# Third and fourth Strassen product exchanged in the later three token blocks of the first input phase of a pooling-mixer kernel

## Chip, cores and metric

The kernel runs on one core of a Trainium2 chip. The metric is the device time of one execution in microseconds (us); lower is better. The engines are named as in the profile: PE (matrix multiply), PEld (its weight load), DVE (vector), ACT (scalar), POOL (GpSimd) and SP, which here only issues DMAs. Each engine runs its own instructions strictly in order, so an instruction that waits holds up everything behind it on its engine.

## What is computed

With these sizes there is one layer, and it is the pooling mixer: 4096 tokens of 1024 channels.

```python
normed = rms_norm(x, norm_w)
u, gate = split(normed @ in_w, 2)            # 1024 -> 2048
pooled[g] = trailing_mean(u[g], (2, 4, 8, 16)[g]) - u[g]      # 4 groups of 256 channels
y = (pooled @ group_w + group_b) * scale * silu(gate)
out = rms_norm(x + y @ out_w, final_norm_w)
```

All arrays are float32. The group map is folded into the input weights at the start, and the pooling works on the result.

## The kernel before, in words

**Three phases.** The list `steps` (lines 949 to 951) holds them one behind the other. Phase "a" multiplies the normalised input by half of the input weights (512 gate columns and 512 folded value columns), in four blocks of 1024 tokens; phase "b" does the same for the other half of the weights from operands that phase "a" saved in HBM (`sd`); phase "o" is the output projection with the residual and the final norm, in eight blocks of 512 tokens.

**Seven products a block.** Each block is a 2x2 block product done by Strassen-Winograd in seven products, P1 to P7, each of 512x512x512. An operand is used as a high part and a low part (float32 split in two float32r numbers), and a product is the sum of three: high by high, high by low, low by high. So `product_in` (line 576) issues 2 halves h of the inner dimension x 4 channel tiles x 2 x 3 = 48 matmuls of 128x128 by 128x512, into four PSUM banks. In P1 the four banks are finished one after the other; in all other products half h=0 goes over all four banks first, then half h=1, so that bank 0 is finished after 5/8 of the product and bank 3 at its end. P1, P2, P7 and P4 use banks 0 to 3, P6, P5 and P3 use banks 4 to 7 (`bank_of`, line 574, and `sets_of`, line 976). P2 adds to what P1 left in banks 0 to 3, and P6, P5 and P3 add to a copy of it that ACT makes in banks 4 to 7.

**Operands.** The input block is in four quarters, "11", "12", "21", "22" (two token halves by two channel halves), each of two tiles of 128x1024 (512 KB). In phase "a" each tile is loaded from the transposed input by SP (`load_x`, line 480), multiplied on DVE by the token's reciprocal root mean square (`normalize`, line 454, traced as L148), and combined on DVE (`add` L142, `sub` L145): "21" becomes 11-21, the operand of P7; a new pair "2" becomes 22-21, the operand of P6; 11+2 is that of P5, 12-2 (`form_s4`, line 548) that of P3. `split` (line 153) then writes one of four operand buffers `op`: ACT writes the high part (L151), DVE the low part, source minus high (L145, `op<-st,op`). In phase "a" the operands of P1, P2, P7 and P4 are also saved to `sd`, each by a DMA that ACT issues (L476).

**Order around the change.** The order of one block is `ORDER_IN` = P1, P2, P6, P7, P5, P4, P3. In the loop from line 1193 on, step n loads for step n+3, forms the operand of step n+2, splits the operand of step n+1 and runs product n. In block b > 0 of phase "a", the step of P1 first normalises all four tiles of 21 and 22 (`normalize_a2`, line 526, called at line 1212), then forms P6's operand (four subtractions, `form_in`), and then splits P2's operand. Where `normal` (line 1213) holds, `form` comes behind the split instead. `evict_in` (line 699) empties the banks: P2's by ACT with SiLU into two tiles, P6's and P7's by ACT copies, P5's and P4's by DVE additions. `pool` (line 617) does the trailing means of an earlier product pair on DVE, multiplies by the gate and stores the result to `yd` (L685, issued by SP). Squares for the next block's norms run on ACT (L407), and the reciprocal roots go through HBM (`rd`) to be spread over partitions (L420, L452, issued by POOL). `save_t3` (line 273, called in block 2 behind P6) makes a weight difference that phase "b" needs.

Tiles come from two pools (`st`, `vt`), handed out oldest first, so what is given back when decides which tile is used next. A scheduler in the framework chooses the order on each engine from the program order; `issue_after` holds an instruction behind a named one.

**At the end** (lines 1259 to 1280) stand 36 matmuls behind the last product: four groups of nine with different access patterns, into banks that nothing reads.

Of the kernel before, what the change touches and what calls it, by code (L numbers as in the profile page):

```python
# [15 lines left out]
P = 128  # L16
# [4 lines left out]
NB = S // TB  # L21
NK = D // P
TO = 512
NBO = S // TO
# [5 lines left out]

P1, P2, P3, P4, P5, P6, P7 = range(1, 8)
ORDER_IN = (P1, P2, P6, P7, P5, P4, P3)
ORDER_OUT = (P1, P7, P6, P2, P5, P4, P3)


# [25 lines left out]
def kernel(  # L61
# [32 lines left out]
    nc = tc.nc  # L94
# [14 lines left out]
    w = {i: new_w(i) for i in (P1, P2, P6, P7)}  # L109
# [28 lines left out]
    def give(ap):  # L138
        next(p for p in (st, vt, early, early5) if id(ap) in p.used).give(ap)
# [4 lines left out]
    def sub(dst, a, b):  # L144
        return nc.vector.tensor_tensor(out=dst, in0=a, in1=b, op=ALU.subtract)  # L145
# [188 lines left out]
    latest = [None]  # L334
# [119 lines left out]
    def normalize(b, half, u):  # L454
        mul(u, u, rstd[b][:, half].unsqueeze(1).to_broadcast([P, 2, H]))
# [24 lines left out]
    def load_x(b, half, kh):  # L480
        us = []
        for h in range(2):
            u = take()
            k = 4 * kh + 2 * h
            nc.sync.dma_start(out=u, in_=xt[2 * b + 1 - half, :, k : k + 2, :])
            us.append(u)
        return us

    def load_saved(b, i):
        us = []  # L490
        for h in range(2):
            u = take()
            nc.sync.dma_start(out=u, in_=sd[b][i][h])
            us.append(u)
        return us

    def load_in(q, b, i):
        s = xs[b]
        if i == P1:
            s["11"] = load_saved(b, P1) if q else load_x(b, 0, 0)  # L500
        elif i == P2:
            s["12"] = load_saved(b, P2) if q else load_x(b, 0, 1)
        elif i == P6:
            s["21"] = load_saved(b, P7) if q else load_x(b, 1, 0)
            s["22"] = load_saved(b, P4) if q else load_x(b, 1, 1)

    def form_in(q, b, i):

        s = xs[b]
        if i in (P1, P2):  # L510
            if q == 0:
                for u in s["11" if i == P1 else "12"]:
                    normalize(b, 0, u)
        elif i == P6:
            s["2"] = [take() for _ in range(2)]
            for h in range(2):
                if q == 0:
                    sub(s["21"][h], s["11"][h], s["21"][h])
                sub(s["2"][h], s["22"][h], s["21"][h])
        elif i == P5:  # L520
            for h in range(2):
                add(s["11"][h], s["2"][h], s["11"][h])
            for u in s.pop("2"):
                give(u)

    def normalize_a2(b):
        for h in range(2):
            normalize(b, 1, xs[b]["21"][h])
            normalize(b, 1, xs[b]["22"][h])
        give(rstd.pop(b))  # L530

    def split_in(q, b, i):
        s = xs[b]
        key = {P1: "11", P2: "12", P6: "2", P7: "21", P5: "11", P4: "22", P3: "12"}[i]
        later = q == 0 and b == 0 and i in (P1, P2)
        t = split_halves(s[key], None if q or later else sd[b].get(i), b == 0)
        if later:
            stores.extend(zip(sd[0][i], s[key]))
        if i == P6 and (q or b):
            form_s4(b)  # L540
        if i not in (P1, P2, P6):
            for u in s.pop(key):
                give(u)
        return t
# [401 lines left out]

    steps = [("a", b, i) for b in range(NB) for i in ORDER_IN]
    steps += [("b", b, i) for b in range(NB) for i in ORDER_IN]  # L950
    steps += [("o", b, i) for b in range(NBO) for i in ORDER_OUT]
    split_up = {}
# [1 line left out]
    def step(n):  # L954
        return steps[n] if n < len(steps) else (None, 0, 0)
# [20 lines left out]
    def sets_of(kind, b):  # L976
        if kind == "o":
            r = 3 * b
            p = [banks[2 * ((r + j) % 4) : 2 * ((r + j) % 4) + 2] for j in range(4)]
            return {"x": p[0], "v": p[1], "y": p[2], "spare": p[3][0]}  # L980
        return {"x": banks[0:4], "v": banks[0:4], "y": banks[4:8]}
# [198 lines left out]
    def row_plan(b):  # L1180
        if b == 0:
            return (
                {P6: range(4), P7: (4, 5), P5: (6, 7)},
                {P7: range(4), P5: (4, 5), P4: (6, 7)},
            )
        return (
            {P1: (0, 1), P2: (2, 3), P6: (4, 5), P7: (6, 7)},
            {P6: (0, 1), P7: (2, 3), P5: (4, 5), P4: (6, 7)},
        )

    scales = {}
# [1 line left out]
    for n in range(2, len(steps)):  # L1193
        kind, b, i = steps[n]
        ahead = kind == "a" and b + 1 < NB
        keep[0] = 5 if kind == "b" and b == NB - 1 else 3
        advance("load", n, load, load_reach)
        if ahead:
            rows, squares = row_plan(b)
            for half, rs in scales.items():  # L1200
                store_rs(b + 1, half, rs)
                load_rstd(b + 1, half)
            scales.clear()
            for j in squares.get(i, ()):
                with tc.issue_after(evicted[0]):
                    square_row(b + 1, j // 4, j % 4)
                if j % 4 == 3:
                    scales[j // 4] = stats(b + 1, j // 4)
            for j in rows.get(i, ()):
                load_row(b + 1, j // 4, j % 4, early if b == 0 and i == P6 else None)  # L1210
        if kind == "a" and b > 0 and i == P1:
            normalize_a2(b)
        normal = kind == "a" and step(n + 2)[2] in (P1, P2)
        if n > 2 and not normal:
            form(n + 2)
        advance("split", n, split_step, split_reach)
        if normal:
            with tc.issue_after(latest_split[0]):
                form(n + 2)
        if n == 2:  # L1220
            with tc.issue_after(first_saves[0]):
                for place, u in stores:
                    nc.gpsimd.dma_start(out=place, in_=u)
            for place, u in stores:
                if id(u) in early5.used:
                    give(u)
            form_s4(0)
            form(n + 2)
        if kind == "a" and b == 0:
            with tc.issue_after(latest_split[0]):  # L1230
                rest_of_first(n)
        pool_due(n)
        since = n - (NB - 1) * len(ORDER_IN) - 2
        if 0 <= since < len(ORDER_IN):
            form_wb(ORDER_IN[since])
        run(n)
        if kind == "a" and b == 2 and i == P6:
            save_t3()
        if 0 <= since < len(ORDER_IN):
            with tc.issue_after(evicted[0]):  # L1240
                split_wb(ORDER_IN[since])
        if 0 <= since + 1 < len(ORDER_IN):
            load_wb(ORDER_IN[since + 1])
        if kind in ("a", "b"):
            pool_later(n)
            if kind == "a":
                pool_due(n)
            if kind == "b" and b == NB - 1:
                load_w(wod, i)
            if kind == "b" and b in (1, 2) and i == P5:  # L1250
                make_wo(b - 1)
            if kind == "b" and b == NB - 1 and i == P3:
                f = take("p (a b) -> p a b", a=2)
                nc.sync.dma_start(
                    out=f.rearrange("p a b -> p (a b)"), in_=final_w.partition_broadcast(P)
                )
                fw.append(f)

    sets = sets_of("o", NBO - 1)
    left, right = ops[0], w[P1][0]  # L1260
    ways = (
        lambda r: r[:, 0:256].rearrange("p (s a) -> p a s", s=2),
        lambda r: r.rearrange("p (s a) -> p a s", s=2)[:, 0:128],
        lambda r: r[:, 0:256],
        lambda r: r.rearrange("p (m s a) -> p m a s", m=2, s=2),
    )
    with tc.issue_after(latest[0]):
        for c, way in enumerate(ways):
            for j in range(9):
                q, part = divmod(j, 3)  # L1270
                r = way(right[:, (0, 1, 0)[part], j % 2])
                bank = sets["x"][c % 2]
                ps = bank if c == 3 else bank[:, 0:256]
                k = 8 * (part == 2) + q
                nc.tensor.matmul(  # L1275
                    ps.rearrange("p (m a s) -> p m a s", m=2, s=2) if c == 3 else
                    ps.rearrange("p (a s) -> p a s", s=2) if c < 2 else ps,
                    left[:, k * P : (k + 1) * P], r, start=j == 0, stop=j == 8,
                    skip_group_check=True,
                )  # L1280


# [50 lines left out]
```

## Time and profile before

| what | value |
|---|---|
| median of 3 runs | 921.17 us (918.97 to 922.02) |
| the profiled execution's own time | 921.6 us |
| its span, first to last instruction | 919.8 us |
| PE busy | 910.0 us, 99% |
| PEld busy | 793.3 us, 86% |
| DVE busy | 702.7 us, 76% |
| ACT busy | 458.2 us, 50% |
| HBM traffic | 177.02 MB moved, mean 192 GB/s |

In a line of the timeline stand: start, duration, engine, line of the kernel, operation, output<-inputs without buffer numbers, shape, and the count of merged instructions; in square brackets how long the engine was idle just before and who ended it. Neighbouring instructions of one kind are merged; a DVE instruction of 128x1024 lasts 1.22 us but the next starts 1.14 us after it. A matmul's end is modelled, and a few matmul records are missing, so the count of a merged line may be a little short of 48 a product. In the list of waits stand: who waited for whom, us in total, times, the longest.

### The profile page before, as it was taken

The numbers are of one execution on the slowest core, as the hardware profiler recorded it, in microseconds if no ns is written. First come the engines' busy times: TensorE is split into PE (matmuls) and PEld (weight loads), VectorE is DVE, ScalarE is ACT, GpSimd is POOL, SyncE is SP. The second block draws the span as 40 slices with busy tenths as digits, with TensorE's granted clock in tenths as the row PEclk, the third lists the DMA queues.
The fourth block names the chain that finished last, engine by engine and source line by source line (L and its number), as shares of the span: only waits on it lengthen the run. The fifth ranks groups of instructions, "written<-read, shape, count | busy, mean of one in ns | idle before, by whom it ended". The sixth has DMA issues, their size and how long they took to land.

```text
span 919.8 us, 11280 instructions
## 1 busy us (share of the span) xinstructions
PE 910.0 (99%) x4248; PEld 793.3 (86%) x4248; DVE 702.7 (76%) x769; ACT 458.2 (50%) x741; POOL 51.6 (6%) x130
## 2 busy tenths in 40 slices
PE   9999999999989999999999999999999999999999
PEld 7888888878878888888888888888888888888888
DVE  3898993795697997496686588589988677676675
ACT  6869447347345565346345545654424424324333
POOL 0023101001100000000000000000001001001010
DMA  9986666565756626116604725746656446356122
GB/s 342 402 313 212 268 237 202 184 248 205 252 229 238 219 109 216 42 46 229 251 37 134 275 92 195 244 149 203 233 178 230 147 150 229 122 199 210 42 92 92
DMA packets 66518, 177.02 MB, mean 192 GB/s; under 512 B 6048, under 2 KB 23840, under 8 KB 66464
## 3 DMA queue, kind: packets, MB, share of 16 engines
q1 hardware_dynamic: 59888, 154.78, 47.4%
q10 hardware_dynamic: 4176, 13.65, 3.7%
q0 software_dynamic: 2400, 7.88, 2.5%
q8 instruction: 33, 0.54, 0.2%
q14 instruction: 21, 0.17, 0.1%
HBM read 115.45 MB, written 60.83 MB: 192 GB/s over the span
## 4 chain that ended last, share of the span: by engine, by line
PE 79%; DVE 9%; DMA 6%; ACT 4%; issue 2%; SPq 0%; POOL 0%; DVEq 0%; ACTq 0%; POOLq 0%
PE bank L570 78%; DMA early<-in_wut 2%; DVE st L148 2%; DVE op L145 2%; DMA st<-in_x 2%; DMA st<-rd 1%; DMA rd<-rs 1%; DVE vt L142 1%; DVE st L145 1%; ACT op L151 1%; ACT early L407 1%; DVE st L142 1%; ACT st L407 1%; ACT vt L407 1%; PE bank L1275 1%
## 5 line engine op out<-in xcount | busy, mean ns | idle before, releaser
L570 PE MATMUL bank<-op,w 128*128 128x512 f32 x2688 | 582.3, 379 | 6.4 <-DVE op L145 5.7
L570 PEld LDWEIGHTS bank<-op,w 128*128 128x128 f32 x2688 | 507.5, 189 | 80.6 <-DVE op L145 7.8
L570 PE MATMUL bank<-w,op 128*128 128x512 f32 (+1 forms) x1356 | 290.3, 377 | 0.0
L570 PEld LDWEIGHTS bank<-w,op 128*128 128x128 f32 x1356 | 254.6, 189 | 35.8
L151 ACT ACTIVATE op<-st 128x1024 fp32r<-128x1024 f32 x126 | 132.4, 1052 | 167.1 <-PE bank L570 150.3
L145 DVE TENSOR_TENSOR op<-st,op 128x1024 fp32r<-128x1024 f32 x126 | 152.9, 1221 | 69.7 <-ACT op L151 69.4
L151 ACT ACTIVATE op<-vt 128x1024 fp32r<-128x1024 f32 x40 | 42.2, 1056 | 76.4 <-PE bank L570 66.3
L151 ACT ACTIVATE vt<-bank 128x512 f32<-128x512 f32 x102 | 58.5, 593 | 37.0 <-PE bank L570 35.0
L913 DVE TENSOR_TENSOR st<-bank,st 128x512 f32<-128x512 f32 x60 | 41.0, 686 | 29.3 <-PE bank L570 29.1
L145 DVE TENSOR_TENSOR st<-st,st 128x1024 f32<-128x1024 f32 x38 | 46.0, 1222 | 20.6 <-DMA st<-wvd 9.2
L145 DVE TENSOR_TENSOR op<-vt,op 128x1024 fp32r<-128x1024 f32 x40 | 48.8, 1221 | 7.8 <-ACT op L151 7.6
L193 POOL TENSOR_SCALAR oms<-oss 128x2 f32<-128x2 f32 x14 | 9.2, 659 | 607.1 <-ACT st L802 601.0
L151 ACT ACTIVATE bank<-bank 128x512 f32<-128x512 f32 x48 | 27.9, 581 | 26.9 <-PE bank L570 21.5
L142 DVE TENSOR_TENSOR vt<-bank,vt 128x512 f32<-128x512 f32 (+1 forms) x55 | 35.9, 678 | 2.2 <-PE bank L570 2.2
L651 DVE TENSOR_TENSOR_SCAN vt<-vt,bf 128x512 f32<-128x512 f32 x28 | 34.5, 1269 | 0.2 <-ACT vt L151 0.2
L913 DVE TENSOR_TENSOR vt<-bank,vt 128x512 f32<-128x512 f32 (+1 forms) x37 | 24.8, 673 | 12.0 <-PE bank L570 11.7
L145 DVE TENSOR_TENSOR w<-st,w 128x1024 fp32r<-128x1024 f32 x20 | 24.2, 1220 | 12.3 <-ACT w L151 12.3
L673 DVE SCALAR_TENSOR_TENSOR vt<-vt,vt 128x1024 f32<-128x1024 f32 x24 | 29.1, 1214 | 0.0
L148 DVE TENSOR_TENSOR st<-st,st 128x1024 f32<-128x1024 f32 (+1 forms) x19 | 21.7, 1163 | 9.7 <-DMA st<-rd 9.0
L151 ACT ACTIVATE w<-st 128x1024 fp32r<-128x1024 f32 x20 | 20.9, 1055 | 16.2 <-PE bank L570 14.9
L806 DVE SCALAR_TENSOR_TENSOR st<-st,ors,st 128x1024 f32<-128x1024 f32 x17 | 21.4, 1281 | 6.1 <-POOL ors L211 6.1
L151 ACT ACTIVATE vt<-vt 128x1024 f32<-128x1024 f32 (+1 forms) x12 | 11.8, 985 | 25.2 <-DVE vt L142 21.6
(132 smaller groups left out, 570.9 us busy)
## 6 DMA issues: line engine op xcount, KB each, us to landing
st<-in_x SPq DMA_DIRECT2D x33, 512.0 KB, 5.1
st<-sd SPq DMA_DIRECT2D x29, 512.0 KB, 4.8
st<-in_xt SPq DMA_DIRECT2D x25, 512.0 KB, 6.7
vt<-in_x SPq DMA_DIRECT2D x24, 512.0 KB, 4.6
sd<-st ACTq DMA_DIRECT2D x19, 512.0 KB, 4.4
yd<-vt SPq DMA_DIRECT2D x19, 512.0 KB, 2.9
st<-yd SPq DMA_DIRECT2D x19, 512.0 KB, 4.4
out<-st SPq DMA_DIRECT2D x17, 512.0 KB, 4.2
```

Of the source, the lines that this page charges most:

```text
L142: nc.vector.tensor_tensor(out=dst, in0=a, in1=b, op=ALU.add)
L145: return nc.vector.tensor_tensor(out=dst, in0=a, in1=b, op=ALU.subtract)
L148: nc.vector.tensor_tensor(out=dst, in0=a, in1=b, op=ALU.mult)
L151: return nc.scalar.activation(dst, src, func)
L193: nc.gpsimd.tensor_scalar(out=ms, in0=ss, scalar1=1.0 / D, scalar2=EPS, op0=ALU.mult, op1=ALU.add)
L407: nc.scalar.activation(u[:, 0], u[:, 0], AF.Square, accum_out=sums[b, half][:, j : j + 1])
L570: latest[0] = nc.tensor.matmul(ps, a, b, start=start and n == 0, stop=stop and n == 2, skip_group_check=True).ins
L651: nc.vector.tensor_tensor_scan(s[:, j, at:end], v[:, j, at:end], v[:, j, at - win : end - win], sums_of[j] if sums_of else 0.0, ALU.add, A ...
L673: nc.vector.scalar_tensor_tensor(out=s[:, :, at : at + H], in0=s[:, :, at : at + H], scalar=1.0 / win, in1=v[:, :, HIST:], op0=ALU.mult, o ...
L806: nc.vector.scalar_tensor_tensor(out=us[j], in0=us[j], scalar=rs[:, j : j + 1], in1=fw[0], op0=ALU.mult, op1=ALU.mult,)
L913: partial["added"] = nc.vector.tensor_tensor(out=dst, in0=src, in1=dst, op=ALU.add).ins
L1275: nc.tensor.matmul(ps.rearrange("p (m a s) -> p m a s", m=2, s=2) if c == 3 else ps.rearrange("p (a s) -> p a s", s=2) if c < 2 else ps, l ...
```

## The change

Blocks 1 to 3 of phase "a" use the order P1, P2, P7, P6, P5, P4, P3; block 0 and the other phases keep theirs. `normalize_a2` is gone: the two tiles of 21 are normalised when P7's operand is formed, those of 22 when P6's is. For P7, P6 and P5 of these blocks, `form` now comes behind the split of the next step's operand (`normal`). 21 is loaded at P7's place and 22 at P6's, 21 is given back behind P6's split, and the loads and squares of the next block's rows keep their places by position. `save_t3` stands behind P6 as before, which is now the fourth product. The 36 matmuls at the end are removed. On DVE the order changes and the amount does not: every normalisation, subtraction and split is still there.

```diff
+ORDER_LATER = (P1, P2, P7, P6, P5, P4, P3)
...
+    def swapped(q, b):
+        return q == 0 and b > 0
...
+        elif i == P7 and swapped(q, b):
+            s["21"] = load_x(b, 1, 0)
         elif i == P6:
-            s["21"] = load_saved(b, P7) if q else load_x(b, 1, 0)
+            if not swapped(q, b):
+                s["21"] = load_saved(b, P7) if q else load_x(b, 1, 0)
             s["22"] = load_saved(b, P4) if q else load_x(b, 1, 1)
...
+        elif i == P7 and swapped(q, b):
+            for h in range(2):
+                normalize(b, 1, s["21"][h])
+            for h in range(2):
+                sub(s["21"][h], s["11"][h], s["21"][h])
         elif i == P6:
             s["2"] = [take() for _ in range(2)]
             for h in range(2):
                 if q == 0:
-                    sub(s["21"][h], s["11"][h], s["21"][h])
+                    normalize(b, 1, s["22"][h])
                 sub(s["2"][h], s["22"][h], s["21"][h])
+            if q == 0:
+                give(rstd.pop(b))
...
-    def normalize_a2(b):
-        for h in range(2):
-            normalize(b, 1, xs[b]["21"][h])
-            normalize(b, 1, xs[b]["22"][h])
-        give(rstd.pop(b))
...
-        if i not in (P1, P2, P6):
+        if i == P6 and swapped(q, b):
+            for u in s.pop("21"):
+                give(u)
+        elif i not in (P1, P2, P6) and not (i == P7 and swapped(q, b)):
...
-    steps = [("a", b, i) for b in range(NB) for i in ORDER_IN]
+    steps = [("a", b, i) for b in range(NB) for i in (ORDER_LATER if b else ORDER_IN)]
...
-        if kind == "a" and b > 0 and i == P1:
-            normalize_a2(b)
-        normal = kind == "a" and step(n + 2)[2] in (P1, P2)
+        ahead_of = step(n + 2)
+        normal = kind == "a" and ahead_of[2] in (P1, P2) or (
+            ahead_of[0] == "a" and ahead_of[1] > 0 and ahead_of[2] in (P7, P6, P5)
+        )
...
-    with tc.issue_after(latest[0]):
-        for c, way in enumerate(ways):
-            for j in range(9):
...
```

More of the change, by code (lines that the diff above doesn't have):

```diff
@@ L1186, in row_plan @@
         return (
-            {P1: (0, 1), P2: (2, 3), P6: (4, 5), P7: (6, 7)},
-            {P6: (0, 1), P7: (2, 3), P5: (4, 5), P4: (6, 7)},
+            {P1: (0, 1), P2: (2, 3), P7: (4, 5), P6: (6, 7)},
+            {P7: (0, 1), P6: (2, 3), P5: (4, 5), P4: (6, 7)},
         )
@@ L1257 @@
                 fw.append(f)
[L1259 to L1266, printed above, removed]
-    with tc.issue_after(latest[0]):
-        for c, way in enumerate(ways):
-            for j in range(9):
[L1270 to L1280, printed above, removed]
 def kernel(**inputs):
```

## The prediction

> **What bounds the kernel now.** I read the page first.
>
> ```profile
> span 919.8 us, 11280 instructions
> PE 910.0 (99%) x4248; PEld 793.3 (86%) x4248; DVE 702.7 (76%) x769; ACT 458.2 (50%) x741; POOL 51.6 (6%) x130
> ```
>
> PE is the bound: whatever doesn't shorten PE's idle time brings nothing. So the next view is PE's timeline, merged, whose brackets give its stops, and the list of PE's waits.
>
> ```profile
> 57.82 61.56 PE L570 MATMUL bank<-op,w 128*128 128x512 f32 x284 [0.58 <-DVE op L145]
> 120.17 72.79 PE L570 MATMUL bank<-op,w 128*128 128x512 f32 x336 [0.79 <-DVE op L145]
> 194.72 62.43 PE L570 MATMUL bank<-op,w 128*128 128x512 f32 x288 [1.76 <-DVE op L145]
> 257.90 10.63 PE L570 MATMUL bank<-op,w 128*128 128x512 f32 x48 [0.75 <-DVE op L145]
> 270.39 149.84 PE L570 MATMUL bank<-op,w 128*128 128x512 f32 x693 [1.86 <-DVE op L145]
> ...
> PE bank L570 <- DVE op L145: 5.7, 5, 1.9
> ```
>
> Five stops, all for the low part of an operand (L145). The row at 194.72 holds 288 matmuls, six products of 48, in 62.43 us: 10.40 us a product, and 1.30 us for the six matmuls of one bank and one half. Counting products puts the stops: 0.58 before P6 of block 0 (not touched), 0.79, 1.76 and 1.86 before P2 of blocks 1, 2 and 3, and 0.75 before P1 of block 3. The four in the changed blocks sum to **5.16 us**. After 270.39 PE has no more.
>
> Why DVE is late shows in its timeline during P1 of block 2 (P1 ends at 194.72 - 1.76 = 192.96), and ACT's beside it.
>
> ```profile
> 172.50 1.23 DVE L148 TENSOR_TENSOR st<-st,st 128x1024 f32<-128x1024 f32 x1 [3.94 <-DMA st<-rd]
> ...
> 180.96 2.35 DVE L145 TENSOR_TENSOR op<-st,op 128x1024 fp32r<-128x1024 f32 x2
> 183.23 2.35 DVE L148 TENSOR_TENSOR st<-st,st 128x1024 f32<-128x1024 f32 x2
> 185.50 1.22 DVE L148 TENSOR_TENSOR vt<-vt,st 128x1024 f32<-128x1024 f32 x1
> 186.63 1.22 DVE L148 TENSOR_TENSOR st<-st,st 128x1024 f32<-128x1024 f32 x1
> 187.77 1.22 DVE L148 TENSOR_TENSOR vt<-vt,st 128x1024 f32<-128x1024 f32 x1
> 188.90 2.36 DVE L145 TENSOR_TENSOR st<-st,st 128x1024 f32<-128x1024 f32 x2
> 191.18 2.36 DVE L145 TENSOR_TENSOR st<-vt,st 128x1024 f32<-128x1024 f32 x2
> 193.45 2.36 DVE L145 TENSOR_TENSOR op<-st,op 128x1024 fp32r<-128x1024 f32 x2
> 195.72 1.22 DVE L145 TENSOR_TENSOR vt<-vt 128x1024 f32<-128x1024 f32 x1
> 203.86 1.41 DVE L681 SCALAR_TENSOR_TENSOR st<-vt,colt,st 128x512 f32<-128x512 f32 x2
> ...
> 184.48 1.06 ACT L151 ACTIVATE op<-st 128x1024 fp32r<-128x1024 f32 x1 [5.29 <-DVE st L148]
> 186.87 1.08 ACT L151 ACTIVATE op<-st 128x1024 fp32r<-128x1024 f32 x1
> 209.88 1.09 ACT L151 ACTIVATE st<-bank 128x512 f32<-128x512 f32 x2 [3.65 <-DVE st L142]
> ```
>
> DVE runs without a gap. The pair at 183.23 normalises P2's operand; ACT has its high parts at 185.54 and 187.95. But the low parts start only at 193.45, because three normalisations and four subtractions for the products behind P2 stand ahead. From 183.23 to 193.45 are nine operations: 1.136 us each.
>
> **The change, part by part.** I use before's clock for each block, and the order in which the changed program issues on each engine.
>
> *Taken from in front of P2's low parts.* They now follow P2's two normalisations directly. Block 2: seven operations less, 7 x 1.136 = 7.95, so 193.45 becomes 185.50 for the first (its high part is done at 185.54), and 187.95 to 189.1 for the second. P2 needs the first at 192.96: 6.3 us to spare where 1.76 lacked. Block 1:
>
> ```profile
> 107.54 6.90 DVE L148 TENSOR_TENSOR st<-st,vt 128x1024 f32<-128x1024 f32 x6
> 118.89 2.36 DVE L145 TENSOR_TENSOR op<-st,op 128x1024 fp32r<-128x1024 f32 x2
> 129.31 1.42 DVE L681 SCALAR_TENSOR_TENSOR st<-vt,colt,st 128x512 f32<-128x512 f32 x2
> ...
> 110.72 1.05 ACT L151 ACTIVATE op<-st 128x1024 fp32r<-128x1024 f32 x1
> 133.68 1.09 ACT L151 ACTIVATE st<-bank 128x512 f32<-128x512 f32 x2 [2.00 <-DMA yd<-st]
> ```
>
> Eight operations leave the front (four of the six at 107.54, four subtractions): 118.89 - 9.09 = 109.8, the second behind ACT's high part at 111.77, done by 112.9. P2 needs them at 120.17 - 0.79 = 119.38. Block 3 is like block 2, with the same seven operations. So **0.79 + 1.76 + 1.86 = 4.41 us** go.
>
> *P1 of block 3* stopped for another reason.
>
> ```profile
> 248.18 1.23 DVE L148 TENSOR_TENSOR st<-st,st 128x1024 f32<-128x1024 f32 x1 [5.07 <-DMA st<-rd]
> 256.63 2.35 DVE L145 TENSOR_TENSOR op<-st,op 128x1024 fp32r<-128x1024 f32 x2
> ```
>
> One normalisation of 21 had been put early in DVE's queue, and waited 5.07 us for the second half of the reciprocal roots, with the additions that empty P4's banks and P1's low parts (256.63) behind it. With `normalize_a2` gone it stands behind P2's low parts. P1's low parts can come up to 5.07 + 1.14 us earlier, until P4's banks set the pace; 0.75 was missing. **0.75 us** go. Block 2 had the same wait (172.50, 3.94 us); nothing stopped there, so it is slack.
>
> *What is late next: P7.* DVE has four operations less ahead of P7's low parts than it had ahead of P6's (22's two normalisations and P6's two subtractions follow later): 4.54 us. The whole queue up to the end of `pool` (203.86 + 1.41 = 205.27) ends at 200.73, P7's low parts sooner, and P7 starts at 192.96 + 10.40 = 203.36. Nothing.
>
> *P6.* From 200.73 follow two normalisations, two subtractions, two for `form_s4` and two low parts: 9.1 us, 209.8. ACT must first copy P2's banks, square two rows and write the high parts, 4 x 1.05 = 4.2 us behind the copies (206.4 by the longest store, next paragraph), so the last low part ends by 211.8. P6 starts at 203.36 + 10.40 = 213.76. Nothing, under 2.0 us of cover; beyond it each us late costs one.
>
> *P7 in P2's banks.* This wait is new: P7 now writes banks 0 to 3 straight behind P2, so each bank must be copied out by then. Bank k is written at 203.36 + 1.30 k and was finished at 199.46 + 1.30 k: 3.90 us for a copy of 0.6. But banks 2 and 3 go into a tile that `pool` has just stored, so their copy waits for the store to land: in before they came at 209.88 and 133.68.
>
> ```profile
> DMA to landing us min/median/max: 2.6/2.9/4.5
> ```
>
> This row is for the stores to `yd` (L685). `pool` ends at 200.73 in block 2; landing at 203.6 (205.2 by the longest), copy done 204.2 (205.8); PE needs bank 2 at 205.96. In block 1 `pool` ends at 130.73 - 4.54 + 0.8 for ACT's late high part = 127.0, copy done 130.5 (132.1), needed at 119.38 + 10.40 + 2.60 = 132.38. The first two of `pool`'s outputs are stored earlier, and in block 3 the target is a tile whose store was issued more than a product earlier. ACT's triggers for saving 22, which wait for its normalisations, now stand among these copies: they hold ACT till 203.0 in block 2 and 129.3 in block 1, before the landing. I take nothing; ends 0 and, if the copies keep before's clock, 6.4 (below).
>
> The Trainium skill, "PSUM — Partial Sum Buffer", in its summary of rules, tells to read PSUM during a matmul only in another bank than the one it writes; by that the exchange is the wrong way round, since two products in a row now share banks. What it would cost is the second rival.
>
> *P5 in P6's banks* likewise follows directly: 3.90 us for each copy, into tiles that no store holds, behind at most 1 us of a split. Nothing; up to 1 us in all.
>
> *SP and POOL.* 21 and 22 were loaded three steps ahead and are needed later than before. `save_t3` moves one product later, and DVE waits for its loads:
>
> ```profile
> 220.13 1.23 DVE L145 TENSOR_TENSOR st<-st,st 128x1024 f32<-128x1024 f32 x1 [4.89 <-DMA st<-wvd]
> 228.04 1.23 DVE L145 TENSOR_TENSOR st<-st,st 128x1024 f32<-128x1024 f32 x1 [4.35 <-DMA st<-wvd]
> ```
>
> In before the second ends at 229.27, 13.7 us behind P6's end (194.72 + 20.80 = 215.52). P6 now ends a product later, at 192.17 + 31.20 = 223.37 on the changed kernel's clock, so the second ends near 237. Behind it on DVE wait the additions that empty P5's banks and P3's low parts, needed when P3 starts at 223.37 + 20.80 = 244.2, and behind those the operand of P1 of block 3 at 254.6. It fits; nothing.
>
> *Phase "b".* PE arrives 5.16 us earlier there. DVE runs without a gap from 302.81 to the low parts of P6 of its block 0:
>
> ```profile
> 302.06 1.32 ACT L223 ACTIVATE w<-vt,colt 128x512 fp32r<-128x512 f32 x2
> 302.81 1.42 DVE L224 SCALAR_TENSOR_TENSOR w<-vt,colt,w 128x512 fp32r<-128x512 f32 x2 [0.49 <-ACT w L223]
> 351.35 2.35 DVE L145 TENSOR_TENSOR op<-vt,op 128x1024 fp32r<-128x1024 f32 x2
> ```
>
> PE needs the first at 270.39 + 8 x 10.40 = 353.6, it is written at 352.57: 1 us of slack, less than 5.16. But the run starts when ACT, behind the copies of the fourth product's banks, gets to the weights (302.06), and those move with PE; and the new order puts four operations that stood ahead of these low parts (4 x 1.14 us) behind them. Nothing.
>
> *The 36 matmuls at the end.*
>
> ```profile
> 912.69 5.19 PE L1275 MATMUL bank<-w,op 128*128 128x256 f32 x36
> 915.70 0.81 SPq L890 DMA_DIRECT2D out<-vt  x2
> ...
> out<-vt SPq DMA_DIRECT2D x2, 128.0 KB, 2.2
> ```
>
> The chain of waits ends in them, but they end at 917.88, and the last store, issued by 916.1, lands 2.2 later, at 918.3. Removing them brings nothing, and no row makes it cost anything.
>
> **Sum:** 4.41 + 0.75 = 5.16 us. The profiled execution took 921.6 (1.8 around its span), so 916.4; it is 0.4 above the median of the runs, for which I say **916.0 us**.
>
> **The rivals.**
>
> 1. *A part comes back* at P6, P5 or P7's banks: ACT has more in front of P6's high parts than I counted, or a store takes longer. 1 to 3 us back: 917 to 919.
> 2. *P7 waits for P2's banks and the change loses.* If the copies of banks 2 stay where before had them, they end at 134.28 and 210.48 against 132.38 and 205.96: 1.9 + 4.5 = 6.4 back against 5.16, so 922.9 on the profiled execution, 922.4 by the median. It decides at the moment `pool`'s last store of a block lands: over 2.0 us (2.60 less a copy) behind the start of P7, each us costs one. For it: the copies were the last thing late in both blocks. Against it: DVE reaches the store 4.5 us sooner.
> 3. *Phase "b" swallows it*: the gapless run of DVE keeps its clock, PE waits 4.1 of the 5.16 there, 920.1. Against it: both points above.
> 4. *The stops are not DVE's order but buffers*: four operand buffers, too few. Then they stay: 921.2. Against it: ACT had written its half of the same buffers by 187.95, five us before DVE came. The Trainium skill, "Perfetto Trace Analysis", in its optimization strategy, says that the same gap coming again can mean that too little SBUF or PSUM is there for the next tile; this row speaks against it. That the change doesn't do what it says gives the same time; the issue order of the changed program shows it.
>
> **How the numbers follow.** My forecast 0.66, with 0 to 0.8 given back; rival 1 0.12; rival 2 0.10, half of it at its price and half with stores that land later still; rival 3 0.05; rival 4 0.03; more gained than counted (a better end, or the slack of block 2) 0.04. About 0.3%, 2.8 us, is what a measurement can tell from no change, so faster means under 918.4: the forecast, the odd gain and half of rival 1, 0.76; slower, over 923.9, is the dearer half of rival 2, 0.05; within, 0.19. The range is 914.0 (1.5 under, the spread of the runs, with a little more gained) to 919.8 (rival 1 and its upper end).
>
> **What would show it.** PE's timeline with stops only before 57.82, and one row from there over all of phase "a". P2's low parts some 6 us ahead of P1's end in each block. The copies of P2's banks 2 and 3 ended within 2.6 us of P7's start; a stop of PE there with ACT as releaser is rivals 1 and 2. No stop at P6 of phase "b"'s block 0 (rival 3). The end still on the stores.

## The result and the profile after

The changed kernel took 916.62 us (median of 6 runs, 915.44 to 917.58) against 921.60 us for the kernel before (6 runs, 918.97 to 923.11): ratio 0.9947, 95% interval 0.9932 to 0.9963, so faster by half a per cent. The forecast was 916.0. A second set of runs of the same program gave 917.41 (9 runs, 915.60 to 919.88; ratio 0.9951, 0.9933 to 0.9968); experiment 6 comes back to that wider scatter.

The profiled execution took 917.32 us. Its page begins so; PE is still the bound.

```profile
span 915.6 us, 11210 instructions
...
PE 904.4 (99%) x4212; PEld 789.0 (86%) x4212; DVE 703.5 (77%) x769; ACT 457.5 (50%) x741; POOL 52.6 (6%) x130
```

PE's timeline, merged; the brackets are its stops and what ended them.

```profile
58.26 197.54 PE L581 MATMUL bank<-op,w 128*128 128x512 f32 x914 [0.58 <-DVE op L146]
256.76 183.59 PE L581 MATMUL bank<-op,w 128*128 128x512 f32 x848 [0.96 <-DVE op L146]
```

From 58.26 one row runs through P2 of blocks 1 and 2: their stops of 0.79 and 1.76 are gone, and so is the 1.86 before P2 of block 3. But a row still begins before P1 of block 3, with a stop of **0.96 us** where before had 0.75. It also begins at another point: before's was at the second matmul of P1, this one at the eighth, where the low part of the second half is first used (P1 takes both halves of a bank in turn).

DVE's timeline during P1 of block 2 shows the cure. The pair at 177.45 normalises P2's operand:

```profile
177.45 2.35 DVE L149 TENSOR_TENSOR st<-st,vt 128x1024 f32<-128x1024 f32 x2
179.79 1.23 DVE L146 TENSOR_TENSOR op<-st,op 128x1024 fp32r<-128x1024 f32 x1
183.38 1.23 DVE L146 TENSOR_TENSOR op<-st,op 128x1024 fp32r<-128x1024 f32 x1 [2.37 <-ACT op L152]
184.53 1.22 DVE L149 TENSOR_TENSOR vt<-vt,vt 128x1024 f32<-128x1024 f32 x1
```

The first low part follows at 179.79, 2.34 us behind the start of the pair instead of 10.22. The second waits 2.37 for ACT's high part, not for DVE's queue.

What stands before P1 of block 3 is another wait than before's. DVE's timeline, and SP's beside it:

```profile
233.47 1.23 DVE L146 TENSOR_TENSOR st<-st,st 128x1024 f32<-128x1024 f32 x1 [5.34 <-DMA st<-wvd]
...
242.49 1.23 DVE L149 TENSOR_TENSOR st<-st,vt 128x1024 f32<-128x1024 f32 x1 [3.07 <-DMA st<-in_xt]
...
255.49 1.22 DVE L146 TENSOR_TENSOR op<-st,op 128x1024 fp32r<-128x1024 f32 x1
```

```profile
222.43 0.32 SPq L283 DMA_DIRECT2D t3d<-st  x1
...
227.62 0.32 SPq L280 DMA_DIRECT2D st<-wvd  x1
...
234.72 0.33 SPq L283 DMA_DIRECT2D t3d<-st  x1
235.14 4.63 SPq L486 DMA_DIRECT2D st<-in_xt  x4
```

`save_t3` works with two tiles, twice. The first store to `t3d` goes out at 222.43; the second load into that tile can go only when it has landed (227.62), the second subtraction comes at 233.47, and the second store at 234.72. The changed program loads P1's operand of block 3 into these same two tiles, so its loads stand behind that store (235.14), and DVE idles 3.07 us for the first of them. From 242.49 on DVE is nearly full; P1's second low part comes at 255.49 and ends at 256.71, and PE goes on at 256.76.

There is a smaller wait at P7, too short for the merged timeline. ACT's copies of P2's banks 2 and 3 in blocks 1, 2 and 3 (in block 3 the first of the two):

```profile
130.87 1.08 ACT L152 ACTIVATE st<-bank 128x512 f32<-128x512 f32 x2 [1.43 <-DMA yd<-st]
...
201.38 0.60 ACT L152 ACTIVATE st<-bank 128x512 f32<-128x512 f32 x1 [0.85 <-DMA yd<-st]
...
278.20 0.60 ACT L152 ACTIVATE st<-bank 128x512 f32<-128x512 f32 x1 [3.92 <-DVE st L149]
```

In block 3 the copy ends at 278.80 and the thirteenth matmul of P7, its first in bank 2, starts at 278.86, 0.41 us behind the twelfth where 0.22 is usual.

**The account closes.** Counted from the starts of single matmuls (0.216 us apart), a stop costs more than its bracket: the next matmul starts 0.16 us later than the bracket says, and the one behind it 0.10 later again. So before's four stops cost 0.95 + 1.93 + 0.92 + 2.03 + 4 x 0.10 = 6.2 us. The changed kernel's cost 1.12 + 0.19 + 2 x 0.10 = 1.5. It also reached the stop in block 0 0.44 later (58.26 against 57.82), a wait for the first loads; in the runs below that stop lies anywhere from 57.86 to 58.77, so this part is scatter and not the change. 6.2 - 1.5 - 0.4 = 4.3, and the profiled times differ by 921.60 - 917.32 = 4.28.

### The profile page after: what moved, and what is told of

Same layout as the page of the kernel before. It is cut to its first block, busy times and chain, and to the rows that moved or that the text cites. A ratio compares the mean times of both kernels' runs of the same rounds, so it can differ in the third digit from the quotient of the medians.

```text
span 915.6 us, 11210 instructions
## 1 busy us (share of the span) xinstructions
PE 904.4 (99%) x4212; PEld 789.0 (86%) x4212; DVE 703.5 (77%) x769; ACT 457.5 (50%) x741; POOL 52.6 (6%) x130
## 4 chain that ended last, share of the span: by engine, by line
PE 88%; DMA 5%; DVE 3%; ACT 2%; issue 1%; SPq 0%; DVEq 0%; ACTq 0%
PE bank L581 88%; DMA early<-in_wut 2%; DMA st<-in_x 1%; DMA st<-wvd 1%; DMA st<-in_xt 1%; DVE op L146 1%; DMA t3d<-st 1%; PE bank L374 0%; DVE st L146 0%; DVE st L149 0%; ACT early L408 0%; ACT op L152 0%; DVE st L143 0%; DVE vt L143 0%; DVE vt L146 0%
## 5 line engine op out<-in xcount | busy, mean ns | idle before, releaser
L146 DVE TENSOR_TENSOR st<-st,st 128x1024 f32<-128x1024 f32 x35 | 42.5, 1221 | 19.3 <-DMA st<-sd 8.6
L143 DVE TENSOR_TENSOR vt<-bank,vt 128x512 f32<-128x512 f32 (+1 forms) x51 | 33.2, 678 | 1.6 <-PE bank L581 1.6
L924 DVE TENSOR_TENSOR vt<-bank,vt 128x512 f32<-128x512 f32 (+1 forms) x37 | 24.8, 673 | 12.0 <-PE bank L581 11.7
L149 DVE TENSOR_TENSOR st<-st,vt 128x1024 f32<-128x1024 f32 x23 | 27.2, 1219 | 3.1 <-DMA st<-in_xt 3.1
L152 ACT ACTIVATE st<-bank 128x512 f32<-128x512 f32 x30 | 17.5, 595 | 22.7 <-PE bank L581 10.8
```

What stands on the lines that cost most here:

```text
L143: nc.vector.tensor_tensor(out=dst, in0=a, in1=b, op=ALU.add)
L149: nc.vector.tensor_tensor(out=dst, in0=a, in1=b, op=ALU.mult)
L152: return nc.scalar.activation(dst, src, func)
L924: partial["added"] = nc.vector.tensor_tensor(out=dst, in0=src, in1=dst, op=ALU.add).ins
```

## The experiments

Theory A: the stops before P2 came from the order of DVE's queue alone; what remains comes from `save_t3`, which holds the operand of P1 of block 3, and from P7 following P2 in the same banks. The rivals: the exchange of products itself removes the stops; DVE's load in the fourth product makes the new one; the banks have cover enough; the 36 matmuls at the end counted. The ratios are against before, run on the same chip.

**1. The queue move without the exchange.** Before's order of products, with P6's four normalisations and four subtractions behind P2's low parts:

```diff
-        if kind == "a" and b > 0 and i == P1:
-            normalize_a2(b)
-        normal = kind == "a" and step(n + 2)[2] in (P1, P2)
+        behind_split = kind == "a" and b > 0 and i == P1
+        normal = behind_split or kind == "a" and step(n + 2)[2] in (P1, P2)
...
             with tc.issue_after(latest_split[0]):
+                if behind_split:
+                    normalize_a2(b)
                 form(n + 2)
```

> The kernel before, its order of products and its save_t3 kept (and the 36 matmuls at the end); only the four normalisations and four subtractions for P6 are put behind the low parts of P2 in the later three blocks. Theory A (the stops before P2 are the order of DVE's queue and nothing else): the stops of 0.79, 1.76 and 1.86 go, and 0.75 before P1 of block 3 too, since the reciprocal roots are no longer waited for in front; P6's low parts had 2.25 to 2.5 us to spare, and PE comes up to 1.86 earlier, so 0.4 to 1.7 are left: no stop, 916.0 to 916.6 profiled, level with the changed kernel or 0.5 to 1 us under it. Rival (the exchange is needed: P6 takes eight operations and comes too early): 1 to 3 us of stops before P6 of blocks 1 to 3, 918 to 920.

916.91 us (6 runs, 915.75 to 917.12), ratio 0.9933 (0.9917 to 0.9949); profiled 915.75. PE's timeline has one row from block 0 to 440 us:

```profile
57.86 382.42 PE L570 MATMUL bank<-op,w 128*128 128x512 f32 x1769 [0.58 <-DVE op L145]
```

All four stops are gone with before's products and before's place of `save_t3`. So the exchange isn't needed, and the 0.75 before P1 of block 3 was the early normalisation's wait, as predicted. P6's cover held.

**2. The exchange without the queue move.** The changed order of products, with all eight operations ahead of P2's low parts again:

```diff
...
+        first = kind == "a" and b > 0 and i == P1
+        if first:
+            normalize_a2(b)
+        formed = kind == "a" and b > 0 and i == P2
...
-        if n > 2 and not normal:
+        if n > 2 and not normal and not formed:
             form(n + 2)
+        if first:
+            form(n + 3)
```

> The changed kernel's order of products, with the four normalisations and four subtractions put ahead of P2's low parts again, as the kernel before has them; save_t3 behind the fourth product. Theory A (order of DVE's queue): the three stops before P2 are back, 0.8, 1.8 and 1.9 us (together 4 to 5), 920.5 to 922 profiled. Rival (the order of products, or the sets of banks, set the stops): they stay away, 916 to 918.

928.16 us (6 runs, 924.59 to 930.37), ratio **1.0056** (1.0034 to 1.0078): slower than before. PE's timeline:

```profile
121.28 13.00 PE L581 MATMUL bank<-op,w 128*128 128x512 f32 x59 [1.22 <-DVE op L146]
137.04 74.47 PE L581 MATMUL bank<-op,w 128*128 128x512 f32 x336 [2.76 <-ACT st L152]
211.91 50.99 PE L581 MATMUL bank<-op,w 128*128 128x512 f32 x235 [0.40 <-ACT st L152]
264.37 9.33 PE L581 MATMUL bank<-op,w 128*128 128x512 f32 x42 [1.46 <-DVE op L146]
276.86 163.40 PE L581 MATMUL bank<-op,w 128*128 128x512 f32 x748 [3.16 <-DVE op L146]
```

The stops before P2 are back in blocks 1 and 3 (1.22, 3.16); in block 2 PE had by then lost enough elsewhere. The rows at 137.04 and 211.91 are new: PE stops inside P7, and ACT's copy of P2's bank ends the stop. They are the prediction's second rival, met here. The 1.46 before P1 of block 3 shows the chain of the changed kernel's 0.96 again: `save_t3`, a product later here too, subtracts at 241.94, and P1's operand waits for its load until 250.09.

```profile
241.94 1.23 DVE L146 TENSOR_TENSOR st<-st,st 128x1024 f32<-128x1024 f32 x1 [6.72 <-DMA st<-wvd]
...
250.09 1.23 DVE L149 TENSOR_TENSOR st<-st,vt 128x1024 f32<-128x1024 f32 x1 [2.20 <-DMA st<-in_xt]
```

So the exchange without the queue move, with `save_t3` a product later, makes the kernel about 6 us slower (928.16 against 922.42 for the kernel before on that chip); how much of that is the exchange by itself isn't separated. The loss is larger than I expected (920.5 to 922), since I had left out the bank waits and what long stops cost beyond their length (last section).

**3. `save_t3` behind the third product again.** One line of the changed kernel:

```diff
-        if kind == "a" and b == 2 and i == P6:
+        if kind == "a" and b == 2 and i == P7:
             save_t3()
```

> The changed kernel (profiled 917.3 us, median 916.6), with save_t3 behind the third product of block 2 again (P7) instead of the fourth. Theory A (the stop of 0.96 us before P1 of block 3 comes from save_t3 a product later: the tiles of P1's operand are those that save_t3 holds, so their loads come behind its second store): the stop falls under 0.2, the operand's normalisations come some 4 us earlier than 242.49 and 245.91, the stop of 0.3 us at P7 of block 3 goes with it, 915.7 to 916.2 profiled. Theory B (that stop comes from DVE's load in the fourth product, the additions that empty P4's banks above all): it stays at 0.7 to 1.0, no change. Theory C: save_t3's waits on DVE now stand ahead of P6's or P5's low parts of block 2, which have 5 to 10 us of cover: a new stop there of 1 us or more.

915.92 us (6 runs, 915.66 to 917.25), ratio 0.9927 (0.9909 to 0.9944); profiled 916.53, a little over what I expected. PE's timeline, DVE's and ACT's:

```profile
133.03 307.18 PE L581 MATMUL bank<-op,w 128*128 128x512 f32 x1422 [0.61 <-ACT st L152]
```

```profile
236.57 2.36 DVE L149 TENSOR_TENSOR st<-st,vt 128x1024 f32<-128x1024 f32 x2
```

```profile
132.38 1.09 ACT L152 ACTIVATE st<-bank 128x512 f32<-128x512 f32 x2 [1.58 <-DMA yd<-st]
```

P1's operand is normalised at 236.57 instead of 242.49 and 245.91; the stop of 0.96 is gone, and the 0.3 at P7 of block 3 with it. The additions that empty P4's banks are all still there, so they aren't the cause. Not expected: 0.61 us at P7 of block 1, where a store landed later than in the profile above and the copy ended at 132.98 instead of 131.47. The store was issued later, at 128.69 instead of 127.32, since DVE was that much behind.

**4. `save_t3` in four tiles.** Its place stays behind the fourth product, but all four loads come first:

```diff
+        us = {}
         for h in range(2):
-            us = []
             for k in (h, 2 + h):
-                us.append(take())
-                nc.sync.dma_start(out=us[-1], in_=wvd[k])
+                us[k] = take()
+                nc.sync.dma_start(out=us[k], in_=wvd[k])
+        for h in range(2):
             with tc.issue_after(evicted[0]):
...
```

> The changed kernel, with save_t3 where the change put it, but its four loads in four tiles, ahead of both subtractions, instead of two tiles used twice. Theory A (the second load waits for the first store to land in the same tile, the second subtraction came at 233.47, and P1's operand is loaded into tiles that it still holds): the second subtraction follows the first by less than 3 us, before 226, P1's operand of block 3 is normalised before 240, the stop of 0.96 goes, 916.0 to 916.6 profiled. Rival (the place behind the fourth product itself, whatever the tiles): the stop stays at 0.7 to 1.0.

916.31 us (6 runs, 915.64 to 916.89), ratio 0.9936 (0.9916 to 0.9956). PE and DVE:

```profile
58.43 381.92 PE L582 MATMUL bank<-op,w 128*128 128x512 f32 x1766 [0.58 <-DVE op L146]
```

```profile
222.09 1.23 DVE L146 TENSOR_TENSOR st<-st,st 128x1024 f32<-128x1024 f32 x1 [1.05 <-DMA st<-wvd]
...
236.50 2.35 DVE L149 TENSOR_TENSOR st<-st,vt 128x1024 f32<-128x1024 f32 x2
```

The last subtraction comes at 222.09 instead of 233.47, the operand at 236.50, and the stop is gone. So it isn't the later place as such, but the same tiles used twice, with a store's landing between.

**5. The stores of `save_t3` on POOL's queue.**

```diff
-            nc.sync.dma_start(out=t3d[h], in_=us[0])
+            nc.gpsimd.dma_start(out=t3d[h], in_=us[0])
```

> The changed kernel, with the two stores of save_t3 issued by POOL's queue instead of SP's. Theory A1 (what holds P1's operand of block 3 are the tiles that save_t3 still uses): the loads come no earlier than the second subtraction, at some 234.7, so the stop stays at 0.7 to 1.0: no change, 917.0 to 917.5. Theory A2 (SP's queue stands behind the second store): the loads come several us earlier, the stop goes, 916.0 to 916.4.

923.65 us (12 runs, 922.86 to 925.58), ratio 1.0014 (1.0003 to 1.0026). Neither theory foresaw that. POOL, SP, DVE and PE:

```profile
225.82 0.58 POOL L453 DMA_DIRECT2D vt<-rd  x1 [4.17 <-DMA rd<-rs]
226.40 0.54 POOL L283 DMA_DIRECT2D t3d<-st  x1
```

```profile
233.16 0.32 SPq L280 DMA_DIRECT2D st<-wvd  x1
233.57 12.17 SPq L486 DMA_DIRECT2D st<-in_xt  x6
```

```profile
236.98 1.23 DVE L146 TENSOR_TENSOR st<-st,st 128x1024 f32<-128x1024 f32 x1 [8.62 <-DMA st<-wvd]
...
249.60 1.23 DVE L149 TENSOR_TENSOR st<-st,vt 128x1024 f32<-128x1024 f32 x1 [3.30 <-DMA st<-in_xt]
```

```profile
256.53 0.48 PE L581 MATMUL bank<-op,w 128*128 128x512 f32 x1 [0.70 <-ACT op L152]
261.74 178.60 PE L581 MATMUL bank<-op,w 128*128 128x512 f32 x819 [4.73 <-DVE op L146]
```

On POOL the first store stands behind a load of reciprocal roots that itself waits 4.17 us, so it goes out 4 us later, and everything behind it follows. P1's second normalisation comes 3.7 us later (249.60 against 245.91), and PE's stop grows from 0.96 to 0.70 + 4.73: past its cover, this chain costs PE us for us and more. Still it settles tiles against SP's queue. No store stands in that queue now, and its six loads stretch over 12.17 us all the same; the list of SP's waits from 215 to 250 says for what:

```profile
SPq L486 <- DMA t3d<-st: 3.9, 1, 3.9
SPq L486 <- DVE st L146: 3.7, 1, 3.7
```

One load waits for `save_t3`'s second subtraction (236.98), another for its second store to land. They go out at 238.23 and 244.94 and land 5.6 and 4.6 us later, and just then DVE starts P1's two normalisations (243.94 and 249.60). So it is the tiles, theory A1; only its forecast of no change was wrong.

**6. The changed kernel once more.**

> The changed kernel once more, unaltered, on the chip of the next run. Theory A: the stops follow from the order of the queues, so they are where they were: 0.58 in block 0, 0.2 to 1.0 before P1 of block 3 and 0.1 to 0.4 at P7 of blocks 1 and 3, which hang on when a store or a load lands; 916 to 917.5.

917.41 us, as told at the top; the profiled execution took 915.60. PE and DVE:

```profile
57.98 382.39 PE L581 MATMUL bank<-op,w 128*128 128x512 f32 x1770 [0.58 <-DVE op L146]
```

```profile
233.49 1.23 DVE L146 TENSOR_TENSOR st<-st,st 128x1024 f32<-128x1024 f32 x1 [5.55 <-DMA st<-wvd]
...
240.71 1.23 DVE L149 TENSOR_TENSOR st<-st,vt 128x1024 f32<-128x1024 f32 x1 [1.27 <-DMA st<-in_xt]
```

The second subtraction stands where it did, 233.49. But the loads behind it landed 1.8 us earlier, DVE normalised at 240.71, and there was **no stop** before P1 of block 3, though I expected 0.2 to 1.0. At P7 it lost 0.1 in block 1 and nothing in block 3. So the late `save_t3` leaves a cover near zero, and between these two executions the landing of one load decides what is paid. That accounts for about 1.2 us; what else makes the runs scatter isn't shown, since one execution of each set has a trace. The slowest run, 919.88, has a mean granted clock of 0.996, where the others have 0.997 to 0.999 and most 0.998. An estimate from that: 0.002 x 918 us is 1.8 us of clock missing, which some 3.8 us at 0.52 would make, the clock that the last section finds behind long stops. So that run probably had one such stop; where it stood is open.

**7. Later stores.** Each store of `pool` in the first phase is preceded by two of the same size to scratch:

```diff
+            for more in extra[2 * g : 2 * g + 2] if q == 0 else ():
+                nc.sync.dma_start(out=more, in_=sg)
             nc.sync.dma_start(
                 out=yd[2 * b + 1 - half][:, 2 * grp : 2 * grp + 2, :], in_=sg
             )
```

> The changed kernel, with every store of pool in the first phase preceded by two stores of the same 512 KB to scratch, so that it is issued some 0.8 us later and lands some 2 to 4 later. Theory A (P7 follows P2 in the same banks, and the copies of P2's banks 2 and 3 wait for that store; at 131.47 in block 1 against 132.6 needed, 201.98 against 205.2 in block 2): a stop of 1 to 3 us in P7 of block 1, 0 to 1 in block 2, with ACT as releaser, 918 to 921. Rival (the banks have cover enough, more traffic costs nothing): 917.0 to 917.6, no stop there.

922.29 us (12 runs, 919.94 to 927.18), ratio 1.0004 (0.9985 to 1.0023): the gain is gone. PE and ACT in block 1:

```profile
131.54 3.94 PE L582 MATMUL bank<-op,w 128*128 128x512 f32 x17 [1.84 <-ACT vt L152]
137.18 122.60 PE L582 MATMUL bank<-op,w 128*128 128x512 f32 x566 [1.71 <-ACT st L152]
```

```profile
130.89 0.60 ACT L152 ACTIVATE vt<-bank 128x512 f32<-128x512 f32 x1 [8.92 <-DVE st L149]
...
136.53 1.09 ACT L152 ACTIVATE st<-bank 128x512 f32<-128x512 f32 x2 [1.94 <-DMA yd<-st]
```

Both stops of PE in P7 of block 1 end as ACT finishes a copy of one of P2's banks (131.49 and 137.13). For the first copy the profile names DVE, which happened to end just then; but the instruction waits for the stores from its own tile as well. The stores to `yd` in this stretch:

```profile
L699 SPq DMA_DIRECT2D yd<-vt x1: 776/776/776, 123.5 to 123.5; - x1
L699 SPq DMA_DIRECT2D yd<-st x1: 449/449/449, 130.2 to 130.2; - x1
...
DMA to landing us min/median/max: 6.3/6.8/7.3
```

123.5 + 7.3 is 130.8, and 130.2 + 6.3 is 136.5: each copy starts as its tile's store lands. So P7 in P2's banks is covered by little, and the rival that more traffic costs nothing falls. The two stops are 3.55 us. The other loads are delayed too (a stop of 0.62 stands before P1 of block 3), so the total isn't the price of the banks alone.

**8. The 36 matmuls at the end**, put back into the changed kernel, and taken out of the kernel of experiment 1:

```diff
+    sets = sets_of("o", NBO - 1)
+    left, right = ops[0], w[P1][0]
...
```

> The changed kernel with the 36 matmuls of the kernel before put back at its end. Theory A (the end is set by the landing of the last stores, so these matmuls cost nothing): level with the changed kernel, 917.0 to 917.6 profiled, medians 916.2 to 917.0; the last store issued some 4 us behind the end of the last product, as without them. Rival (they lengthen the end, by up to their own 5.19 us): 918 to 922.

> The run with the queue move alone (before's order of products), now without the 36 matmuls at the end: the change without its exchange. Theory A: as with them, 915.5 to 917 (the run with them gave 916.91, with runs from 915.75 to 917.12), and no stop in the first phase beside 0.58 in block 0. If the exchange brings something that the profile of one run doesn't show, this stays behind the changed kernel with the 36 matmuls in the same call, by more than 1 us.

With them the changed kernel took 917.18 us (7 runs, 915.81 to 918.49; ratio 0.9948, 0.9928 to 0.9968), level with it. Without them the queue move alone took 916.80 (6 runs, 915.22 to 917.72; ratio 0.9941, 0.9920 to 0.9962), level with itself. So they cost nothing that these runs can tell. Both ran on one chip, and the queue move alone isn't behind the changed kernel: beyond the queue move, no run shows the exchange of products to bring anything. That last kernel also shows a stop in the second phase, before P6 of its block 0:

```profile
348.92 91.35 PE L570 MATMUL bank<-op,w 128*128 128x512 f32 x422 [0.66 <-DVE op L145]
```

That is the prediction's third rival in small; the changed kernel's own profile has none there.

**9. The good parts together**: products exchanged in blocks 2 and 3 only, in block 1 the queue move with before's order, and `save_t3` in four tiles.

```diff
...
     def swapped(q, b):
-        return q == 0 and b > 0
+        return q == 0 and b > 1
...
-    steps = [("a", b, i) for b in range(NB) for i in (ORDER_LATER if b else ORDER_IN)]
+    steps = [("a", b, i) for b in range(NB) for i in (ORDER_LATER if b > 1 else ORDER_IN)]
```

> The parts that the runs found good, together: products exchanged in blocks 2 and 3 only, in block 1 the queue move with before's order of products (so that P7 doesn't follow P2 in its banks, where the copies were late by 0.1 to 0.6), and save_t3 in four tiles. Theory A: no stop in the first phase beside 0.58 in block 0; 0.9 to 1.4 under the changed kernel by the trace, 915.5 to 916.3 profiled, so faster than it by little more than the runs scatter. Rival (P6 or P7 of block 1 or 2 now comes late in the mixed order): a stop of 0.5 or more there, 916.5 to 918.

915.88 us (5 runs, 915.38 to 916.35), ratio 0.9932 (0.9912 to 0.9952). The changed kernel on the same chip had 917.41.

```profile
58.54 381.64 PE L585 MATMUL bank<-op,w 128*128 128x512 f32 x1767 [0.58 <-DVE op L146]
```

No matmul of blocks 1 to 3 comes late any more, and the runs lie within 1 us. It is faster than the kernel before. That it is faster than the changed one isn't shown: the medians differ by 1.5 us, but the intervals overlap, and the two profiled executions went the other way (916.07 against 915.60).

## Why the prediction was right, point by point

**The stops before P2: right, and for the reason given.** The 4.41 us went, and experiment 1 separates the causes: the place in DVE's queue does it, the exchange isn't needed. Experiment 2 has two of the three stops back. That the stops might be buffers (rival 4) is refuted: the four operand buffers are the same throughout.

**P1 of block 3: the failed step.** The early normalisation that waits for the reciprocal roots was rightly read as the cause of the 0.75, and that wait went. But of `save_t3` a product later the prediction says "It fits; nothing". It had moved the second subtraction to 237, counted what DVE does behind it, and stopped there. What it left out is that SP loads P1's operand into the tiles which `save_t3` gives back, behind its last store. The subtraction even came earlier than that (233.47), and still the operand came too late. Size: 0.96 us in the profile (1.2 counted from the starts), 0.24 in the run of experiment 8, nothing in experiment 6.

**P7 in P2's banks: taken as 0 within 0 to 6.4; measured 0.3.** In block 2 the copy of bank 2 ended at 201.98 where 204.2 was forecast, in block 1 at 131.47 where it was 130.5. Block 3 was counted safe because its target tile had been stored long before; there ACT's triggers for saving 22 held the copy (278.20, waiting for DVE), a mechanism that the prediction named only for blocks 1 and 2. That block 1 paid nothing in this profile was luck. `pool`'s last store went out at 127.32 in this profile, and between 128.44 and 129.21 in the five others with this order and this queue (experiments 3, 4, 5, 6 and 8); there the copy of bank 2 ended between 132.06 and 132.98, against 132.38 needed by the prediction's reckoning, and P7 of block 1 lost 0.1 to 0.9 us, counted from the starts. With a later `pool` (experiments 2 and 7) the rival decides, as it said. The Trainium skill, "PSUM — Partial Sum Buffer", in its summary of rules, advises to read PSUM during a matmul from a different bank, or at least a different quadrant (the prediction leaves the quadrant out). The exchange lets P7 write the banks that ACT is still copying out for P2; here that shows as waits of PE for a bank's copy, 2.76 and 0.40 us in experiment 2.

**P6, P5, the second phase, the end: right.** No stop there in the changed kernel; the 36 matmuls cost nothing (experiment 8).

**The sum.** 5.16 was too small for what went (6.2, since a stop costs more than its bracket) and too large for what stayed gone: 1.5 came back and the start was 0.44 later. Part of the errors cancel, so it is in part luck that the forecast came within 0.6 us. The profiled execution, 917.32, is the first rival's (917 to 919); the median of 916.62 lies between. Other executions with shorter waits would explain that; experiment 6 shows one.

## What to carry to other kernels

When an in-order engine is late, move in its queue what the next product doesn't need. Here that was enough; the order of the products moved banks and stores with it, and brought nothing more that the runs can tell. Of a step that is moved, follow the tiles it gives back, not only its instructions: who loads into them next, and behind which store. A wait for a DMA with a cover near zero shows in one profile and not in the next, so look at two before calling it gone.

## What the runs showed of the hardware

A long stop of PE costs more than its length. In experiments 2 and 5 the first matmuls behind stops of 2.76, 3.16 and 4.73 us started 0.43 us apart instead of 0.22, for about 3.5 us. Behind stops of 1.84 us and 1.71 (experiment 7) and 1.86 (the kernel before) only the first interval was longer (0.32). Busy time by stretch has, from the left, the stretch, its length, PE's busy time with the count of matmuls, and the granted clock. First experiment 2, then experiment 7.

```profile
137.03:140.56 3.53, 3.52 (x9) 0.52 0.22 51
140.56:144.00 3.44, 3.44 (x17) 1.00 0.67 252
276.85:280.59 3.74, 3.73 (x10) 0.54 0.69 275
```

```profile
137.17:140.70 3.53, 3.52 (x16) 1.00 0.57 185
```

Nine matmuls in 3.53 us, where an undisturbed stretch of the same length holds sixteen: some 1.6 us on top of each such stop, and part of why experiment 2 lost more than its brackets. The Trainium skill, "TensorE: Matmul & The Clock Gate", in its part on the clock gate, tells of a clock at half rate after an idle window of about 3.4 us and of as long a time to come back. The way back agrees (3.5 us at 0.52); but here 2.76 us of idle were already enough, and the measurement decides.
